# One small load split over two issuing queues, in a kernel that streams 285 MB

## The chip, the cores and the metric

The kernel runs on one core of a Trainium2 chip. The metric is the time of one execution on the device in microseconds. The profile gives a span, from the first to the last instruction, which is about 1.7 us shorter. Faster or slower would need a difference of 2%, 13 us.

## The reference

```python
def setup_inputs():
    B, H, W = 4, 4224, 4224
    return {"x": np.random.randn(B, H, W).astype(np.float32)}

def reference(x):
    ps = np.cumsum(np.cumsum(x, axis=1), axis=2)
    diag = np.diagonal(ps, axis1=1, axis2=2)
    return np.cumsum(diag, axis=1).astype(np.float32)
```

Each element of x has to be read once: 285.47 MB. The output is 4 x 4224 numbers.

## The kernel before

Strips of 768 rows (6 per partition) are loaded by GpSimd, which casts them from fp32 to bf16 on the way. There are three strip buffers. Each strip is summed along rows (VectorE and ScalarE) and along columns (TensorE). The last 384 rows of the last matrix are handled by blocks of 128 rows, and their last 384 columns, the *head*, are loaded first of all, in fp32, by SyncE.

```python
    HC = GW                      # 384
    NH = N - HC
    src = x[LB, T0:N, :].rearrange("(h p) w -> p h w", p=P)
    src_a = src[:, 0:2, :]
    head = last.tile([P, F, HC], FP32, name="head")        # F = 3 blocks
    nc.sync.dma_start(out=head, in_=src[:, :, NH:N])
    ...
    prefetched = []
    for i in range(NBUF):        # 3 strips ahead
        t = strip_tile()
        load_rows(t, 0, i * F2 * P)                        # nc.gpsimd.dma_start
        prefetched.append(t)
    ...                          # constants: some 25 GpSimd instructions
    row_sums(hs, head)           # the head's first reader, on VectorE
    for h in range(F):
        w = GW - h * P
        masked(hmu[:, h, :w], head[:, h, HC - w :], um1[:, :w], hu[:, h : h + 1])
    ...
    # then for each strip: mask, subtract, row sums (VectorE), column sums (TensorE)
```

Of the kernel before, what the change touches and what calls it, by code (L numbers as in the profile page):

```python
# [17 lines left out]
def kernel(  # L18
# [15 lines left out]
    nc = tc.nc  # L34

    B, H, W = x.shape
    N = H
# [31 lines left out]
    NH = N - HC  # L69
    src = x[LB, T0:N, :].rearrange("(h p) w -> p h w", p=P)  # L70
    src_a = src[:, 0:2, :]
    head = last.tile([P, F, HC], FP32, name="head")
    nc.sync.dma_start(out=head, in_=src[:, :, NH:N])

    def strip_tile():
        return strips.tile([P, F2, N], BF16, name="strip")
# [21 lines left out]
    def upper_mask(f, c0):  # L98
# [17 lines left out]
        out=um1,  # L116
        in_=um1,
# [13 lines left out]
        out=ident,  # L131
        in_=ident,
# [30 lines left out]
    def between_groups(name, n, turned):  # L163
# [39 lines left out]
        out=weights,  # L203
        in_=weights,
# [12 lines left out]
        out=steps, in_=steps, scalar=2, op=ALU.arith_shift_right  # L217
# [84 lines left out]
    for b in range(B):  # L302
# [90 lines left out]
        if not whole:  # L393
# [9 lines left out]
            for sb, c0, c1 in (  # L403
# [8 lines left out]
                    out=part_b[:, sb, c0:c1],  # L412
                    in_=x[b, r0 : r0 + R, :NH].rearrange("r (k c) -> r k c", k=4)[
                        :, :, c0:c1
                    ],
# [23 lines left out]
        for i, src in enumerate((d, c12[:, 0, :])):  # L439
            nc.vector.tensor_tensor_scan(  # L440
                out=c12[:, i, :],
# [6 lines left out]
        if whole:  # L448
# [4 lines left out]
            out=out[b, :T0].rearrange("(g i) -> g i", i=GW), in_=c12[1:, 1, :]  # L453
# [60 lines left out]
        for k in (1, 0, 2):  # L514
# [3 lines left out]
            out=out[b, T0 : T0 + E0].unsqueeze(0), in_=yl[:, :E0]  # L518
# [34 lines left out]
```

## Time and profile before

| | before |
|---|---|
| time, first three runs | 667.07 us median (667.06 to 667.53) |
| span | 665.4 us |
| read from HBM | 285.47 MB |
| transfer engines busy, 2 to 662 us | full (share 1.01) |
| first byte | 1.8 to 2.0 us |
| head: issued, landed, first read | 0.82, 4.8, 20.27 us |
| last strip data landed | 662.3 us |

The lines behind this table stand in the prediction. Read such a page from the DMA row: as it is full in every slice here, an instruction on another engine can matter only if it moves the beginning or the end of the stream, or makes a hole in it.

### The profile page before, as it was taken

The page shows a single profiled execution, that of the slowest core. Times are in us where ns is not written, and L with a number is a line of the kernel's source. Part 1 is how long each engine was busy: PE and PEld are TensorE (multiplying, and loading weights), DVE is VectorE, ACT ScalarE, POOL GpSimd, SP SyncE. Part 2 cuts the span into 40 slices and gives each one's busy share as a digit, 9 for nine tenths or more (in the row PEclk, how much of TensorE's full clock was granted, in tenths as well). Part 3 has the DMA queues.
Part 4 walks back from the last instruction along what each step waited for, and adds up shares of the span by engine and source line. Part 5 has one row for each costly group of instructions (what it writes and reads, how often), then busy time and mean ns, then how long its engine had stood idle before and what let it go on. Part 6 is the DMA issues. An engine that isn't in the chain of part 4 may idle for free.

```text
span 665.4 us, 2461 instructions
## 1 busy us (share of the span) xinstructions
PE 201.7 (30%) x948; PEld 103.7 (16%) x948; DVE 326.4 (49%) x136; ACT 136.9 (21%) x222; POOL 31.8 (5%) x62
## 2 busy tenths in 40 slices
PE   0081423402007143140200623404032163250418
PEld 0040211201004021120100312202011031120103
DVE  3261625456906153454780524436388243352767
ACT  0001121406300103040630020304063002030434
POOL 6100000000000000000000000000000000001000
PEclk9995857656558585666755957666565586766758
DMA  9999999999999999999999999999999999999998
GB/s 206 219 219 219 219 219 215 212 210 218 219 218 219 219 220 218 218 213 212 216 218 218 217 219 219 218 219 211 215 216 219 219 214 220 216 219 216 214 208 162
DMA packets 7631, 143.25 MB, mean 215 GB/s; under 512 B 536, under 2 KB 1604, under 8 KB 2116
## 3 DMA queue, kind: packets, MB, share of 16 engines
q0 software_dynamic: 7152, 142.44, 99.9%
q1 hardware_dynamic: 468, 0.66, 0.3%
q8 instruction: 7, 0.11, 0.1%
q14 instruction: 4, 0.03, 0.0%
HBM read 285.47 MB, written 0.07 MB: 429 GB/s over the span
## 4 chain that ended last, share of the span: by engine, by line
another core or an unknown queue 44%; DVE 42%; DMA 11%; issue 1%; POOL 0%; PE 0%; DVEq 0%; POOLq 0%
DVE acc L246 27%; DMA strip<-in_x_dram 11%; DVE mu L333 7%; DVE strip L334 7%; DVE c L440 0%; POOL strip L411 0%; DVE rows L348 0%; PE d L226 0%; POOL strip L400 0%; DVE pu L246 0%; PE fin_e L226 0%; DVE c L266 0%; DVE pair L255 0%; PE carry_ps L226 0%
## 5 line engine op out<-in xcount | busy, mean ns | idle before, releaser
L226 PE MATMUL d<-strip,sel 128*33 128x384 bf16 (+1 forms) x603 | 140.7, 408 | 397.9 <-DMA strip<-in_x_dram 397.9
L241 ACT ACTIVATE dump<-strip 128x416 bf16<-128x416 bf16 (+6 forms) x110 | 125.1, 1138 | 520.5 <-DMA strip<-in_x_dram 517.8
L333 DVE TENSOR_TENSOR mu<-strip,um 128x4608 bf16<-128x4608 bf16 (+1 forms) x24 | 52.4, 2183 | 316.4 <-DMA strip<-in_x_dram 316.3
L246 DVE TENSOR_REDUCE acc<-strip 128x6 f32<-128x4608 bf16 (+6 forms) x23 | 196.0, 8523 | 0.8
L226 PEld LDWEIGHTS <-sel 128*33 128x33 bf16 (+1 forms) x849 | 94.9, 112 | 534.1 <-issue 495.9
L226 PE MATMUL d<-mu,sel 128*33 128x384 bf16 (+1 forms) x243 | 48.9, 353 | 45.4 <-DVE mu L333 45.4
L334 DVE TENSOR_TENSOR strip<-strip,mu 128x4608 bf16<-128x4608 bf16 (+1 forms) x24 | 52.4, 2183 | 1.0
L80 POOL DMA_DIRECT2D strip<-in_x_dram x24 | 16.5, 687 | 536.7 <-DVE acc L246 312.3
L241 ACT ACTIVATION_READ_ACCUMULATOR dump<-strip 128x1 f32 x110 | 20.5, 186 | 0.0
L226 PE MATMUL fold<-strip,ident_h 128*128 128x480 bf16 x8 | 3.4, 601 | 10.8 <-DMA strip<-in_x_dram 10.8
L96 DVE MEMSET um<- 128x6144 bf16 x1 | 5.2, 5178 | 1.2 <-issue 1.2
L216 DVE TENSOR_SCALAR steps<-steps 128x128 int32<-128x128 int32 x1 | 0.2, 227 | 11.0 <-POOL steps L215 11.0
L101 POOL TENSOR_SCALAR_AFFINE_SELECT um<-um 128x4608 bf16<-128x4608 bf16 (+1 forms) x2 | 5.2, 2614 | 4.0 <-DVE um L96 4.0
L226 PEld LDWEIGHTS <-ident_h 128*128 128x128 bf16 x21 | 2.2, 113 | 14.8 <-issue 13.8
L411 POOL DMA_DIRECT2D strip<-in_x_dram x5 | 2.7, 552 | 26.5 <-DMA strip<-in_x_dram 26.5
L226 PE MATMUL d<-ones_all,rows 128*33 128x128 f32 (+1 forms) x12 | 2.3, 347 | 5.4 <-DVE rows L348 5.4
L226 PE MATMUL fold_a<-strip,ident_h 128*128 128x512 bf16 x13 | 3.3, 380 | 0.3 <-DMA strip<-in_x_dram 0.3
L246 DVE TENSOR_REDUCE parts<-strip 128x3 f32<-128x3072 bf16 x1 | 3.4, 3352 | 0.0
L400 POOL DMA_DIRECT2D strip<-in_x_dram x2 | 1.4, 714 | 30.8 <-DVE acc L246 30.8
L226 PEld LDWEIGHTS d<-halves,rows 128*33 128x33 f32 (+1 forms) x24 | 2.5, 150 | 0.7 <-issue 0.5
L226 PE MATMUL d<-halves,rows 128*33 128x64 f32 (+1 forms) x24 | 2.6, 284 | 0.0
L348 DVE TENSOR_TENSOR rows<-acc 64x30 f32<-64x30 f32 (+2 forms) x12 | 2.1, 177 | 0.9
(80 smaller groups left out, 34.7 us busy)
## 6 DMA issues: line engine op xcount, KB each, us to landing
strip<-in_x_dram POOLq DMA_DIRECT2D x19, 6336.0 KB, 76.6
strip<-in_x_dram POOLq DMA_DIRECT2D x5, 3168.0 KB, 59.8
strip<-in_x_dram POOLq DMA_DIRECT2D x1, 1152.0 KB, 50.2
strip<-in_x_dram POOLq DMA_DIRECT2D x1, 768.0 KB, 53.3
strip<-in_x_dram POOLq DMA_DIRECT2D x3, 240.0 KB, 54.3
head<-in_x_dram SPq DMA_DIRECT2D x1, 576.0 KB, 4.0
strip<-in_x_dram POOLq DMA_DIRECT2D x1, 176.0 KB, 43.2
strip<-in_x_dram POOLq DMA_DIRECT2D x1, 64.0 KB, 28.6
```

Source lines behind the costliest of these rows:

```text
L80: nc.gpsimd.dma_start(out=o, in_=x[b, r0 : r0 + f * P, :].rearrange("(p f) w -> p f w", f=f))
L96: nc.vector.memset(um_all, 1.0)
L101: nc.gpsimd.affine_select(out=um, in_=um, compare_op=ALU.is_gt, fill=0.0, base=0, pattern=[[-1, f], [1, f * P]], channel_multiplier=-f,)
L216: nc.vector.tensor_single_scalar(out=steps, in_=steps, scalar=2, op=ALU.arith_shift_right)
L226: nc.tensor.matmul(o, lhsT=lhsT, rhs=rhs, start=start, stop=False, skip_group_check=True)
L241: nc.scalar.activation(out=dump[:, :w], in_=src, func=ACT.Copy, accum_out=acc)
L246: nc.vector.reduce_sum(out=acc, in_=src, axis=AX.X)
L333: nc.vector.tensor_mul(out=mu, in0=block, in1=um)
L334: nc.vector.tensor_sub(out=block, in0=block, in1=mu)
L348: nc.vector.tensor_add(out=o, in0=acc[..., 0], in1=acc[..., 1])
L400: nc.gpsimd.dma_start(out=part_a[:, :, c0:c1], in_=src_a[:, :, c0:c1])
L411: nc.gpsimd.dma_start(out=part_b[:, sb, c0:c1], in_=x[b, r0 : r0 + R, :NH].rearrange("r (k c) -> r k c", k=4)[:, :, c0:c1],)
```

## The change

The intent is to spread the first load over two sequencers (the parts of SyncE and ScalarE that issue loads), so that issuing and landing overlap: row blocks 0 and 1 by SyncE, block 2 by ScalarE, which has nothing to do at that time.

```diff
     head = last.tile([P, F, HC], FP32, name="head")
-    nc.sync.dma_start(out=head, in_=src[:, :, NH:N])
+    nc.sync.dma_start(out=head[:, 0:2, :], in_=src[:, 0:2, NH:N])
+    nc.scalar.dma_start(out=head[:, 2, :], in_=src[:, 2, NH:N])
```

## The prediction

> **What bounds the kernel now.** I read the page first: the row of DMA busy shares in 40 slices, the GB/s row, the queue table and the HBM line.
>
> ```profile
> span 665.4 us, 2461 instructions
> ...
> DMA  9999999999999999999999999999999999999998
> GB/s 206 219 219 219 219 219 215 212 210 218 219 218 219 219 220 218 218 213 212 216 218 218 217 219 219 218 219 211 215 216 219 219 214 220 216 219 216 214 208 162
> ...
> q0 software_dynamic: 7152, 142.44, 99.9%
> q1 hardware_dynamic: 468, 0.66, 0.3%
> ...
> HBM read 285.47 MB, written 0.07 MB: 429 GB/s over the span
> ```
>
> The reader is to see that the transfer engines are at 90% or more in every slice but the last, and that almost all of it is one queue, the casting strip loads that GpSimd issues. The queue that the change touches (q1, SyncE's loads and stores) holds 0.66 MB of 143.25 MB and 0.3% of the engines' time. The GB/s row counts bytes written into the core's memory: a strip is read as 4 bytes and written as 2, so 219 written is 438 read. The input, 4 x 4224 x 4224 x 4 bytes = 285.47 MB, is exactly what the page says was read: each element is read once, and there is nothing to save.
>
> Second, stretches of time at both ends, to see when the transfers begin and stop (columns: stretch, length, busy times of PE, PEld, DVE, ACT and POOL, clock, DMA share, GB/s).
>
> ```profile
> 1.60:1.80 0.20, 0.00 (x0) 0.00 (x0) 0.00 (x0) 0.20 (x1) 0.20 (x1) 1.00 0.00 0
> 1.80:2.00 0.20, 0.00 (x0) 0.00 (x0) 0.00 (x0) 0.20 (x1) 0.20 (x1) 1.00 0.20 61
> 2.00:2.20 0.20, 0.00 (x0) 0.00 (x0) 0.00 (x0) 0.10 (x1) 0.20 (x2) 1.00 1.44 169
> ...
> 2.00:662.00 660.00, 200.76 (x937) 103.05 (x937) 325.05 (x128) 135.07 (x220) 30.93 (x58) 0.66 1.01 217
> ```
>
> No byte moves before 1.8 us; from 2 us to 662 us the share is 1.01, that is full. So the time is about 1.9 us to the first byte, 660.4 us of streaming, and the rest to the end. 285.47 MB in 660.4 us is 432.3 GB/s.
>
> Third, the chain of waits, its first transfer and its end (start, length, what), and two lines of the list of who waited for whom (total, times, longest).
>
> ```profile
> 1.33 33.28 DMA strip<-in_x_dram
> ...
> 619.08 43.23 DMA strip<-in_x_dram
> 662.33 0.40 DVE pair L255 x2
> ```
> ```profile
> DVE mu L333 <- DMA strip<-in_x_dram: 316.3, 20, 19.8
> POOL strip L80 <- DVE acc L246: 312.3, 10, 32.2
> ```
>
> The chain gives VectorE 42% of the span, because each new strip load is issued when VectorE has released a buffer. This is not the bound: VectorE then waits 316.3 us for strips, and GpSimd waits for it only with other strips already queued (a strip load lands 76.6 us after its issue, 2.5 times the 30 us that one strip streams). The queue never runs dry, as the row of nines says. The chain ends in a strip transfer that lands at 662.33 us; 3.1 us of finishing work follow.
>
> Fourth, the timeline of the start, for the first load itself, and the list of issues for its landing (KB each, us to landing).
>
> ```profile
> 0.81 1.28 ACT L241 ACT_TABLE_LOAD   x1 [0.81 <-PEq L537]
> 0.82 0.45 SPq L73 DMA_DIRECT2D head<-in_x_dram  x1
> ...
> 1.33 2.27 POOL L80 DMA_DIRECT2D strip<-in_x_dram  x3 [0.81 <-POOLq L537]
> ...
> 20.27 1.31 DVE L246 TENSOR_REDUCE hs<-head 128x3 f32<-128x1152 f32 x1
> ...
> 34.64 2.56 DVE L333 TENSOR_TENSOR mu<-strip,um 128x4608 bf16<-128x4608 bf16 x1 [11.82 <-DMA strip<-in_x_dram]
> ```
> ```profile
> head<-in_x_dram SPq DMA_DIRECT2D x1, 576.0 KB, 4.0
> ```
>
> The head is issued at 0.82 us and has landed 4.0 us later, at 4.8 us. Its first reader, the row sum on VectorE, starts at 20.27 us with no wait in brackets: it comes after constants that GpSimd was making until 19.1 us. Head data has lain ready for 15.5 us. ScalarE does a table load and then nothing until the first strip lands at 34.6 us.
>
> **What the Trainium skill says.** "DMA: Bandwidth & Descriptors", section "Issuing engines are not separate DMA queues": loads from SyncE, ScalarE and GpSimd run on the same 16 transfer engines, and issuing from several "will only save the time on the sequencer". The trace of before has SyncE's head and GpSimd's strips both moving in the first microseconds, but cannot yet test two such hardware queues. Same page, "Where 436 GB/s comes from": a fabric ceiling of 435.2 GB/s. The 432.3 GB/s worked out above is 99.3% of it: agreement, and nothing left to gain in rate. Same page, "Latency and other measured facts": first byte about 0.6 us for loads issued from SyncE or ScalarE. Here the issue ends at 0.82 + 0.45 = 1.27 us and bytes appear between 1.8 and 2.0 us, so 0.5 to 0.7 us after the end of the issue, or about 1.1 us after its start. "Perfetto Trace Analysis", section "Summary: the profiler window per engine type": the window of such an issue leaves out the data movement. The trace agrees: 0.45 us of window against 4.0 us to landing.
>
> **The change part by part.**
> 1. Removed: one load of 128 x 3 rows of 384 floats (384 runs of 1,536 bytes, 576 KB) from SyncE. Added: one of 256 runs (384 KB) on SyncE, one of 128 runs (192 KB) on ScalarE. Bytes and run length are the same; 0.59 MB at 432 GB/s is 1.4 us of the engines' time in both kernels. Difference in streaming time: 0.
> 2. SyncE's issue: if the 0.45 us were wholly proportional to runs it would become 0.30 us, if fixed it stays 0.45. Nothing else is on SyncE before 517 us. What could matter is only whether the first byte comes sooner: by at most 0.15 us, and this counts only because for a moment the head has the engines to itself (GpSimd's first strip issue lasts from 1.33 to about 2.1 us).
> 3. ScalarE's issue: by the same row 0.3 to 0.45 us, ahead of or behind its table load of 1.28 us (0.81 to 2.09 us). If ahead, the table load ends at about 2.5 us; first use at 34.6 us, slack 32 us. If behind, the third block is issued at 2.1 us and lands by about 2.1 + 4.0 = 6.1 us; first use at 20.27 us, slack 14 us. On the path: 0 in either case.
> 4. Landing of the head: perhaps half a microsecond sooner or later than 4.8 us. The row sum needs all three blocks and still starts at about 20.3 us. On the path: 0.
> 5. Waits: the row sum now waits for two completions, and the end of the program may have one more queue to settle. The last waits of SyncE at the end are 0.2 us each; I put 0 to 0.2 us here, as an estimate from those.
> Sum: -0.15 to +0.2 us, centre 0. 667.07 + 0.03 gives 667.1 us.
>
> **The rivals.**
> - The start gets faster: two sequencers share the issuing, the engines fill sooner, and everything behind moves up. For it: the stream is continuous, so a microsecond gained at the start would come through to the end whole. Against: GpSimd's strips are ready for the engines from about 2 us anyway, and no byte can be moved before the issue and the latency to first byte, which both kernels have. Gain at most 0.15 us: 666.9 us.
> - The two hardware queues beside the strips' queue hold back the first strip: three queues in turn, not two, so a smaller part for strips while the head is moving. For it: the head and strips overlap. Against: the head ends sooner by as much as it takes, and the stream only cares for the sum of bytes. The first strip might land at 34.6 plus or minus 0.5 us; with full queues behind it the end stays. 667.1 us.
> - A fixed price for the first use of ScalarE's queue, at start or end, outside the span: the measured time is 1.7 us more than the span (667.14 against 665.4), which is the size of all such work that before has. One more queue could add some tenths: 667.5 us. Nothing in the profile of before can show it.
> - The head comes late, with VectorE's start held up: it would have to land 15 us later to be seen at all, and another 12 us (the 11.82 us of idle time before the first strip) to reach the strips. Excluded in practice.
>
> **Range and chances.** The three runs of before lie from 667.06 to 667.53 us, so 0.5 us of scatter is ordinary. Adding the -0.15 to +0.5 us of the rivals and a little for another chip or moment (0.1%, 0.7 us, a guess), I take 666.3 to 668.2 us. A step of 2% is 13.3 us, more than nine times the time of all the head's bytes, and nothing here can make it: chances 0.01 faster, 0.98 within 2%, 0.01 slower, the ends left for a disturbed run.
>
> **What would show it right or wrong.** Right: HBM read still 285.47 MB; the row of nines as before; two head issues at about 0.8 us, from SyncE and ScalarE, both landed before 7 us; the row sum of the head at 20.3 us with no wait on a transfer; first strip work at 34.6 us, within 0.5; the last strip landing at 662.3 us, within 0.5. Wrong: a slice with a hole in the DMA row; a strip landing late by the same amount all through; a wait on the head before the row sum; or a span that stays while the measured time rises, which would be the queue's fixed price. A first byte clearly before 1.8 us with the last landing earlier by as much would speak for the first rival.

## The result, and the profile after

The changed kernel took 667.93 us in the median of six runs (667.03 to 668.64), the kernel before 667.18 us in six runs (667.06 to 667.53). The ratio is 1.0009, with a 95% interval from 0.9996 to 1.0022: no difference. (A ratio here is the mean time of one kernel's fast runs over the mean of the other's of the same rounds, so not quite the ratio of the two medians.) The profiled run took 667.05 us, with a span of 665.3 us. The gap between time and span is 1.7 us, as before.

The page after, DMA row, queues (packets, MB, share of the engines' time) and HBM line:

```profile
span 665.3 us, 2463 instructions
...
DMA  9999999999999999999999999999999999999998
...
q1 hardware_dynamic: 340, 0.46, 0.2%
q10 hardware_dynamic: 144, 0.20, 0.2%
...
HBM read 285.47 MB, written 0.07 MB: 429 GB/s over the span
```

A new queue, q10, has taken 0.20 MB from q1. Its 144 packets are 128 runs of the head and 16 more of a few bytes: q1 went from 468 to 340, the total from 7631 to 7647. The DMA row and the bytes read are unchanged.

The timeline of the start, and the first reader of the head and of a strip:

```profile
0.82 0.45 SPq L73 DMA_DIRECT2D head<-in_x_dram  x1
0.82 0.41 ACTq L74 DMA_DIRECT2D head<-in_x_dram  x1
...
1.26 1.28 ACT L242 ACT_TABLE_LOAD   x1 [1.26 <-PEq L538]
1.33 2.27 POOL L81 DMA_DIRECT2D strip<-in_x_dram  x3 [0.81 <-POOLq L538]
...
20.27 1.31 DVE L247 TENSOR_REDUCE hs<-head 128x3 f32<-128x1152 f32 x1
...
34.71 2.56 DVE L334 TENSOR_TENSOR mu<-strip,um 128x4608 bf16<-128x4608 bf16 x1 [11.88 <-DMA strip<-in_x_dram]
```

Both issues begin at 0.82 us. SyncE's takes as long for 256 runs as it took for 384 (0.45 us), and ScalarE needs 0.41 us for 128. ScalarE's table load has moved back by 0.45 us, which delays nothing. The row sum of the head starts at 20.27 us as before.

The landing of the two parts (KB, us from issue), and the two strip transfers at the ends of the chain of waits:

```profile
head<-in_x_dram SPq DMA_DIRECT2D x1, 384.0 KB, 4.1
head<-in_x_dram ACTq DMA_DIRECT2D x1, 192.0 KB, 3.3
```
```profile
1.33 33.35 DMA strip<-in_x_dram
...
618.98 43.22 DMA strip<-in_x_dram
```

The whole head is there at 4.9 us, against 4.8 before: two queues have not brought it sooner. The first strip landed at 34.68 us against 34.61, the last at 662.20 against 662.31 (start and length added, as in the lines above and in those of the prediction).

### The profile page after: what moved, and what is told of

Read it like the earlier page. It is cut to its first block, busy times and chain, and to the rows that moved or that the text cites. A ratio compares the mean times of both kernels' runs of the same rounds, so it can differ in the third digit from the quotient of the medians.

```text
span 665.3 us, 2463 instructions
## 1 busy us (share of the span) xinstructions
PE 197.0 (30%) x948; PEld 101.8 (15%) x948; DVE 326.4 (49%) x136; ACT 136.9 (21%) x222; POOL 31.8 (5%) x62
## 4 chain that ended last, share of the span: by engine, by line
another core or an unknown queue 44%; DVE 42%; DMA 12%; issue 1%; POOL 0%; PE 0%; DVEq 0%; POOLq 0%
DVE acc L247 27%; DMA strip<-in_x_dram 12%; DVE strip L335 7%; DVE mu L334 7%; DVE c L441 0%; POOL strip L412 0%; DVE rows L349 0%; PE d L227 0%; POOL strip L401 0%; DVE pu L247 0%; PE fin_e L227 0%; DVE c L267 0%; DVE pair L256 0%; PE carry_ps L227 0%
## 5 line engine op out<-in xcount | busy, mean ns | idle before, releaser
L227 PE MATMUL d<-strip,sel 128*33 128x384 bf16 (+1 forms) x603 | 137.0, 400 | 401.1 <-DMA strip<-in_x_dram 401.1
L227 PEld LDWEIGHTS <-sel 128*33 128x33 bf16 (+1 forms) x849 | 93.3, 110 | 534.9 <-issue 494.9
L227 PEld LDWEIGHTS d<-ones_all,rows 128*33 128x33 f32 (+1 forms) x12 | 1.4, 131 | 6.8 <-DVE rows L349 5.6
```

Of the source, the lines that this page charges most:

```text
L227: nc.tensor.matmul(o, lhsT=lhsT, rhs=rhs, start=start, stop=False, skip_group_check=True)
```

## The experiments

What was left to explain: whether the 0.75 us between the two medians is real, and whether the time follows the bytes of the head, its landing, or something else. My theory was that of the prediction (a full stream; the head's 1.4 us of bytes cost the same in both kernels, and its landing time costs nothing). The rivals were a price of ScalarE's queue, a price of an additional load, and transfer time at the start that lies idle and hides the head. Eleven runs of kernels were made, each timed in five rounds beside the kernel before.

| run | median, us | lowest to highest, us | ratio to before, 95% interval |
|---|---|---|---|
| before against itself | 668.10 | 667.50 to 669.07 | 1.0005 (0.9991 to 1.0019) |
| changed, again | 667.17 | 667.04 to 668.27 | 0.9998 (0.9985 to 1.0010) |
| changed, third time | 667.17 | 667.11 to 667.38 | 0.9994 (0.9980 to 1.0007) |
| split on SyncE alone | 667.03 | 666.95 to 669.24 | 0.9997 (0.9984 to 1.0010) |
| whole head on ScalarE | 667.34 | 666.99 to 668.42 | 0.9999 (0.9986 to 1.0011) |
| 1.18 MB more at the start | 670.29 | 670.23 to 670.37 | 1.0034 (1.0021 to 1.0046) |
| head issued at 20 us | 668.87 | 668.76 to 668.99 | 1.0013 (0.9999 to 1.0027) |
| no head load | 667.10 | 666.90 to 667.30 | 0.9992 (0.9979 to 1.0004) |
| head on GpSimd's queue | 668.31 | 668.16 to 668.67 | 1.0011 (0.9998 to 1.0023) |
| strips after the head | 670.73 | 670.68 to 670.95 | 1.0047 (1.0035 to 1.0060) |
| first strip's load cut in two | 667.33 | 667.16 to 668.07 | 0.9996 (0.9982 to 1.0009) |

### Are the 0.75 us real?

The kernel before against itself, with no edit:

> The kernel before against itself, to see what scatter a comparison has here. Every theory: ratio 1.000, interval within 0.001 on either side, median 667.1 to 667.3 us. If it comes out at 1.001 (667.9) as the changed kernel did, that 0.75 us is drift and belongs to no kernel.

The changed kernel again and a third time, with no edit:

> The changed kernel again, unaltered. Theory (the load lies off the path, the time is the stream of bytes): ratio 1.000 within 0.0005, median 667.0 to 667.4 us. Rival (ScalarE's queue has a fixed price that four of the six first runs paid): ratio 1.001 to 1.0015, median about 667.9 us, again in two groups (667.0 and 668.2).

> The changed kernel a third time, on whatever chip this is, for the two groups: theory: best runs 667.0 to 667.1, others 1 to 2 us above, as with before; in its profile the work on the first strip and the last transfer are late by the same amount against the best run (34.7 and 662.3 us).

The kernel before, against itself, came out at 1.0005, with a median of 668.10 us for five runs and 667.71 us for the nine beside them. The changed kernel came out at 0.9998 and 0.9994. So the 0.75 us belong to no kernel. Over all comparisons the changed kernel ran 16 times, from 667.03 to 668.64 us with a median of 667.19; the kernel before ran 47 times, from 667.01 to 669.32 us with a median of 667.53. The best runs agree within 0.02 us. Both kernels have runs of 1 to 2 us more, those of before on all three chips, and the expectation of an interval of 0.001 either side was too narrow.

### A price of the queue, or of one more load?

```diff
 # split on SyncE alone
+    nc.sync.dma_start(out=head[:, 0:2, :], in_=src[:, 0:2, NH:N])
+    nc.sync.dma_start(out=head[:, 2, :], in_=src[:, 2, NH:N])
 # whole head on ScalarE
+    nc.scalar.dma_start(out=head, in_=src[:, :, NH:N])
```

> The same split into two blocks and one, both issued by SyncE one after the other; ScalarE issues nothing. Theory: 667.1 us, ratio 1.000. Rival of the queue's price: also 667.1, as no new queue is used. Rival of the additional load (16 more completion packets, two semaphores for the row sum): 667.9 us, ratio 1.001. In the trace the second issue should follow the first by 0.45 us, so the third block lands later than with ScalarE, at about 5 us, still 15 us ahead of its reader.

> The whole head as one load from ScalarE, none from SyncE at the start. Theory: 667.1 us, ratio 1.000, head landed about 4.0 us after its issue, table load of ScalarE moved from 0.81 to 1.26 us. Rival of the queue's price: 667.9 us or more, ratio 1.001, as ScalarE's queue is used and now for all the head's bytes. Rival of the additional load: 667.1 us.

Best runs 666.95 and 666.99 us: neither the new queue nor the additional load has a price that can be seen (the intervals reach some 0.9 us to either side). The two parts on SyncE were issued at 0.82 and 1.31 us, and each landed 3.3 us after its issue, the last at 4.6 us; with ScalarE's help it was 4.9 us, and 4.7 us in the second profile of the changed kernel.

The profiled run of the split on SyncE is worth a look, as it took 669.24 us, while the four timed ones took 666.95 to 667.18. Its chain of waits:

```profile
1.33 35.83 DMA strip<-in_x_dram
...
621.19 43.22 DMA strip<-in_x_dram
```

The first strip landed at 37.16 us, 2.5 us later than in the runs of 667 us, and the last strip data at 664.41, 2.2 us later. All that was lost was lost before the first strip was in. The last microseconds show how (stretches; the last two columns are the share of the 16 engines and GB/s), first of this run, then of the changed kernel at 667.05 us:

```profile
662.50:663.00 0.50, 0.42 (x2) 0.17 (x3) 0.35 (x3) 0.50 (x2) 0.00 (x0) 1.00 0.14 24
663.00:663.50 0.50, 0.50 (x6) 0.39 (x5) 0.00 (x0) 0.12 (x2) 0.00 (x0) 1.00 0.11 19
663.50:664.00 0.50, 0.50 (x8) 0.40 (x6) 0.46 (x3) 0.40 (x1) 0.00 (x0) 1.00 0.08 14
664.00:664.50 0.50, 0.50 (x9) 0.41 (x6) 0.38 (x2) 0.25 (x3) 0.00 (x0) 1.00 0.08 11
```
```profile
662.00:662.50 0.50, 0.41 (x7) 0.18 (x4) 0.43 (x2) 0.30 (x2) 0.00 (x0) 1.00 0.10 13
662.50:663.00 0.50, 0.33 (x6) 0.21 (x6) 0.50 (x5) 0.32 (x2) 0.00 (x0) 1.00 0.00 0
```

One engine of 16 is a share of 0.06. In the slower run about one engine worked alone from 663.5 us on, and the others had finished. In the faster run all were done by 662.5. So a strip is there when the last of 16 engines has its part, and one late engine makes the whole run late.

The transfer records of the packed traces bear this out. They don't name the engine, but a strip's packet (25,344 bytes written) follows the one before it on its engine without a gap, 1.89 us each, so 16 chains can be told apart. This is when the 11th packet of a chain ended: the spread over the 16 chains and the last of them, beside the time of the same run. The last three rows are of runs described below.

| profiled run | spread, us | last end, us | time, us |
|---|---|---|---|
| changed, third time | 0.47 | 25.03 | 667.17 |
| before | 0.52 | 25.02 | 667.14 |
| changed | 0.60 | 25.06 | 667.05 |
| before against itself | 1.19 | 25.98 | 668.20 |
| whole head on ScalarE | 1.74 | 26.31 | 668.42 |
| changed, again | 1.91 | 26.38 | 668.15 |
| split on SyncE | 2.93 | 27.52 | 669.24 |
| no head load | 1.04 | 25.14 | 667.16 |
| head on GpSimd's queue | 0.73 | 26.26 | 668.32 |
| strips after the head | 0.86 | 28.59 | 670.68 |

The time follows the last end: in all ten runs it is 641.7 to 642.2 us more, while the last ends lie 3.6 us apart. The spread alone misleads: without the head it is 1.04 us and nothing is lost, because there the other engines are early and the last one is not late. In the split on SyncE the last engine's first strip packet began at 6.17 us (on the others at 3.6 to 4.3 us), though all packets of the head had ended by 4.29 us on every engine; and in all four slower runs of the first seven the last engine's first strip packet took 2.7 to 2.9 us in place of 1.89.

### What the head's bytes cost

```diff
 # 1.18 MB more at the start: a second load behind the head, into a buffer overwritten later
     nc.sync.dma_start(out=head, in_=src[:, :, NH:N])
+    extra = mup.tile([P, F2, F2 * P], BF16, name="mu6")
+    nc.sync.dma_start(out=extra.bitcast(FP32), in_=x[0, 0:F2 * P, 0:HC].rearrange("(f p) w -> p f w", p=P))
```

> Before, with a second load behind the head on SyncE: 768 runs of 1,536 bytes, 1.18 MB, twice the head's bytes, into a buffer that is overwritten before it is used (results stay right). Theory (bytes count, landing times do not): 1.18 MB at 432.3 GB/s is 2.7 us, so 669.9 us, ratio 1.0041, the whole stream shifted by 2.7 us and no hole in the DMA row. Rival (the start has idle transfer time that hides small loads): under 0.5 us, 667.1 to 667.6 us. Rival (short runs are dearer than their bytes): over 4 us, 671 us or more.

670.29 us, all five runs within 0.14 us, and 3.0 us above the lowest run of before on the same chip (667.25). Bytes alone would make 2.7 us. By the records a packet of 1,536 bytes takes 65 to 78 ns on an engine, and 768 / 16 = 48 of them make 3.1 to 3.7 us, an estimate; the 3.0 us lie between the two reckonings. Taken alone, this run spoke for the prediction and against the rival of idle time at the start. The run without a head, below, shows why it could not tell: the head itself already fills that time. The extra load landed 55.1 us after its issue, and VectorE, which needed that buffer, began on the first strip at 56.56 us in place of 34.64. That lateness of 22 us is not seen in the time.

```diff
 # head issued at 20 us: its load waits for a write that GpSimd makes after its constants
-    nc.sync.dma_start(out=head, in_=src[:, :, NH:N])
     ...
+    nc.gpsimd.memset(head, 0.0)
+    nc.sync.dma_start(out=head, in_=src[:, :, NH:N])
     asum = last.tile([P, 2, 4], FP32, name="asum")
```

> Before, with the head's load held back until GpSimd has made its constants (it writes the head's tile first, so the load waits for it), at about 19 us, in the midst of the strip stream. Theory: the same bytes in the same stream, so as long as the head lands before VectorE's other work runs out of buffers the time stays 667.1 us, ratio 1.000; VectorE's row sum of the head is then held up by a wait for the head that the trace shows, and if this goes past 34.6 us the first strip's work comes late, which the three buffers should absorb up to about 30 us. Rival (the first strip's work is on the path): the time grows by as much as the first strip's work is late. If the head takes turns with the strips' large packets on each engine it could land some 10 to 50 us after its issue; 4 us if not.

The issue list and the timeline of this run, VectorE's row sum with the wait before it and its first work on a strip:

```profile
head<-in_x_dram SPq DMA_DIRECT2D x1, 576.0 KB, 48.0
```
```profile
68.14 1.35 DVE L245 TENSOR_REDUCE hs<-head 128x3 f32<-128x1152 f32 x1 [46.97 <-DMA head<-in_x_dram]
...
70.65 2.55 DVE L334 TENSOR_TENSOR mu<-strip,um 128x4608 bf16<-128x4608 bf16 x1
```

In the midst of the strip stream the head needed 48.0 us to land, not 4. On each engine its 24 packets take turns with strip packets: 24 x (1.89 + 0.08) = 47 us. VectorE began on the first strip 36 us late. Yet the time was 668.87 us, only 1.8 us above the 667.10 us of the next run, which has no head load; 24 packets of 78 ns are 1.9 us. (In its records the last of the 16 chains ended its 11th packet at 24.96 us, and the time is 643.8 us more, not 642: again 1.8 us, put in after the start.) So even here the time follows what the engines have to move, and 36 us of lateness are absorbed by the buffers. But the expected ratio of 1.000 was wrong: bytes that cost nothing at the start cost 1.8 us here.

```diff
 # no head load: results of the last blocks wrong on purpose
-    nc.sync.dma_start(out=head, in_=src[:, :, NH:N])
     ...
+    nc.gpsimd.memset(head, 0.0)
```

> Before without the head's load at all: GpSimd fills the head's tile with zeros, so the last row blocks come out wrong on purpose. Theory of the prediction (the head's 0.59 MB cost 1.4 us of the stream wherever they lie): 667.1 - 1.4 = 665.7 us at best. New theory after the late-head run (the strips' own first packets start only at about 2.8 us, and the head fills engine time that would lie idle): 666.6 to 667.2 us at best. Theory on the scatter (one of the 16 engines now and then starts its strips late while the head's packets are in its way, and the whole stream ends late by that): without the head's load the five runs agree within 0.4 us. Rival on the scatter (the chip or the strips alone): they spread over 1 us or more, as before does.

This run decides it: 667.10 us with no head at all, 666.90 at best, against 667.01 at best for before. The prediction's 1.4 us for the head's bytes would have made it 665.7. The medians of the same rounds differ by more, 667.10 against 667.75 us, and the interval (0.9979 to 1.0004) would by itself allow 1.4 us; but the runs of before include late engines, so I compare the best runs, and the two profiled runs at 667.14 and 667.16 us. (The comparison with the reference passed in spite of the zeros, presumably because the head's part is small beside sums over the whole matrix; so that comparison doesn't guard the head.) Stretches at the start, without the head:

```profile
2.60:2.80 0.20, 0.00 (x0) 0.00 (x0) 0.20 (x1) 0.00 (x0) 0.20 (x1) 1.00 0.00 0
2.80:3.00 0.20, 0.00 (x0) 0.00 (x0) 0.20 (x1) 0.00 (x0) 0.20 (x2) 1.00 7.40 1140
```

GpSimd's strips, issued at 1.32 us, move nothing before 2.8 us. (A long packet is booked in the stretch in which it begins, hence a share over 1.) Bytes of the head move from 1.8 us on. Moreover, the records show that the first strip packet on each engine takes 2.6 us in the median here, where it takes 1.89 us in the kernel before, in which the head has gone ahead of it. So about 0.9 + 0.7 = 1.6 us of each engine's time is there for the head, which needs 24 x 65 to 78 ns = 1.6 to 1.9 us. This is an account by sums, and the chains of packets add to it: on the middle one of the 16 engines the 11th strip packet ended at 24.29 us without the head and at 24.75 with it, on the last one at 25.14 and 25.02. So the head cost most engines about 0.5 us, and nothing on the last one, which sets the time. The first strip's work began at 34.81 us without the head and at 34.64 us with it.

### What of the start counts in full

```diff
 # head on GpSimd's queue, ahead of the strips
-    nc.sync.dma_start(out=head, in_=src[:, :, NH:N])
+    nc.gpsimd.dma_start(out=head, in_=src[:, :, NH:N])
 # strips after the head
     nc.sync.dma_start(out=head, in_=src[:, :, NH:N])
+    probe = last.tile([P, 1], FP32, name="probe")
+    nc.gpsimd.tensor_copy(out=probe, in_=head[:, 2, HC - 1 : HC])
```

> The head issued by GpSimd ahead of the strips, on their queue; SyncE and ScalarE issue nothing at the start. If the idle time before 2.8 us is what the head uses up, this costs the head's own time: 1.4 to 1.9 us above the best runs of before and up to 0.8 us for GpSimd's additional issue ahead of the strips, 668.4 to 669.8 us. If the queue doesn't matter: 667.1 us. Scatter: small, below 0.4 us, if it comes from two queues meeting on an engine.

> Before, but GpSimd reads one column of the head before it issues the first strip, so the strips start when the head has landed, at about 3.5 to 4.8 us. Head and strips never meet on an engine at the start. Stream: later by some 2 to 3 us, 669 to 670.5 us at best. Scatter, if it comes from the meeting: below 0.4 us. If it has another cause: 1 us or more.

On GpSimd's queue the head cost 1.2 us against no head (668.31 against 667.10), a little less than the 1.3 to 2.7 us that I expected: it began at 2.8 us as the strips would have done, and the strips' first issue came 0.9 us later. The timelines show when the strips were issued, first without a head, then with the strips held back until the head was there:

```profile
1.32 2.27 POOL L79 DMA_DIRECT2D strip<-in_x_dram  x3 [0.81 <-POOLq L537]
```
```profile
4.80 0.19 POOL L75 COPY probe<-head 128x1 f32<-128x1 f32 x1 [4.27 <-DMA head<-in_x_dram]
4.92 1.55 POOL L82 DMA_DIRECT2D strip<-in_x_dram  x2
```

4.92 us against 1.32 us is 3.6 us later, and 670.73 against 667.10 us is 3.6 us longer; more than the 2 to 3 us that I expected. So the strips' first issue is on the path: these 3.6 us came through whole, and the head's issue is not on it.

The scatter was nearly gone in the runs in which head and strips did not meet at the start (head late, no head, head on the strips' queue, strips after the head): 20 runs, each kernel's five within 0.51 us. Of the 47 runs of before, 22 were above 667.6 us. But the run with more bytes at the start was within 0.14 us though there they meet, and the third group of the changed kernel within 0.27 us. So the late engine seems to have to do with how the start is laid out, which no run isolates. I had expected the head's packets to be in its way; the split on SyncE, where they had all ended 1.9 us before the late engine's first strip packet began, speaks against that. What makes it late remains open.

### A version that beats both?

```diff
 # first strip's load cut in two
-            load_rows(t, 0, i * F2 * P)
+            nc.gpsimd.dma_start(out=t[:, 0:1, :], in_=rows0[:, 0:1, :])   # for i == 0
+            nc.gpsimd.dma_start(out=t[:, 1:, :], in_=rows0[:, 1:, :])
```

> A try for a version that beats both: before, with the first strip's load cut in two (one row of each partition's six, then the other five), so that GpSimd's first and smaller load may be written out sooner and the strips start before 2.8 us. From the run with the strips issued 3.6 us later, which ended 3.6 us later, the first issue counts in full: if the smaller load takes 0.55 us to issue where the whole one takes 0.75, best runs 666.8 to 666.9 us. Rival (the head fills the time before the strips' first packets, so an earlier start of the strips only displaces the head): 667.0 to 667.1 at best, as before. Rival (runs of 16.9 KB in place of 101 KB, and one more issue): 667.3 us or more at best.

667.16 us at best against 667.20 of before on that chip. GpSimd's first issue took 0.66 us, not 0.55. Nor did the strips start sooner: by the records of its profiled run (668.07 us) their first packet began at 3.96 us, in before at 3.83. So the earlier start that this run was to test did not come about, and what one would be worth is not shown. Nothing is gained, and I have found no version that beats either kernel. With the head removed altogether the best time falls by 0.1 us only; what else it takes away is scatter.

## Why the prediction was right or wrong

The predicted 667.1 us and "within 2%" held: 667.93 us in the first six runs lies in the range, and 667.19 us over all 16.

1. *Streaming time, difference 0*: right. Bytes and the DMA row are the same, and the last strip data landed within 0.1 us of before.
2. *SyncE's issue, 0.30 to 0.45 us*: it is 0.45. The issue is not in proportion to the runs (0.45 us for 384 and for 256, and 0.46 us for 128 in the split on SyncE), so no first byte could come sooner; it is at 1.8 to 2.0 us in both.
3. *ScalarE's issue ahead of its table load, slack of 32 us*: right, as the timeline shows.
4. *Landing within half a microsecond of 4.8 us, off the path*: right (4.9 us), and the late head shows how far off: 48 us to land, and 36 us of lateness not seen.
5. *More to wait for, 0 to 0.2 us*: nothing can be seen; the gap of time and span stayed at 1.7 us.

Two terms were mis-sized without harm to the result. The 1.4 us of engine time for the head's bytes was put into both kernels; at the start it measures 0.1 us between the best runs, in the midst of the stream 1.8 us. As it stood in both kernels, its error cancelled, and the predicted difference did not depend on it. The step that failed is the sentence in the first rival, that the strips "are ready for the engines from about 2 us anyway": alone they start at 2.8 us, and behind the head at 3.8 us. And the scatter of "0.5 us" came from three runs; 47 runs spread over 2.3 us. With the range cut to that first scatter, the median of the first six runs would have been missed.

One reading of the prediction is not shown either. It finds 432.3 GB/s in agreement with a ceiling of 435.2 GB/s, which its page states for the ports of the core's memory. The 432.3 count bytes read; 217 GB/s were written into that memory. That the engines are busy throughout is shown (share 1.01), but not that this ceiling is what limits them.

The rival of three queues in turn named the right place, for it is in the first microseconds that an engine can fall behind. But this occurs in before as well (22 of 47 runs above 667.6 us, against 6 of 16 of the changed kernel), so nothing marks it as an effect of the third queue.

## What to carry to other kernels

In a kernel with a full stream, ask of each load at the start whether it delays the stream's first issue (3.6 us later cost 3.6 us here), and not how fast it lands itself; a small load on a quicker queue before the stream gets going cost 0.1 us between the best runs here, and the same load in the middle cost 1.8 us. To know what a load costs, take it away: the run without the head was worth more than any split of it. Before a difference of a microsecond is explained, run the kernel against itself, and look at when the last of the transfer engines ends.

## What the Trainium skill lacked or had wrong

- "DMA: Bandwidth & Descriptors", section "Queues, rings and completion order", says that an engine takes turns between queues packet by packet. The late head agrees (24 turns beside packets of 1.89 us, 47 us worked out, 48.0 us measured). But the section gives some 9 to 17 descriptors as typical of a packet, where a turn here moved one run of 1,536 bytes; and it lacks the consequence: a small load with short runs, issued into a stream of long ones, took 12 times as long as at the start.
- The same page, "Specifications", gives 512 bytes as the least transfer for line rate. Here runs of 1,536 bytes took 78 ns beside the stream, 19.7 GB/s on an engine (65 ns at the start, 23.6 GB/s), where a strip packet reads 50,688 bytes in 1.886 us, 26.9 GB/s, all counted in bytes read.
- No page that I read shows how one late engine of 16 looks in a profile: there is no hole in the DMA row, only a share near 0.06 in the last microseconds. In the split on SyncE the first strip landed 2.5 us late, the last strip data 2.2 us late, and the run took 669.24 us against 667.1 us.
- No page that I read says whether the issue of a load grows with its runs: SyncE's took 0.45 us for 384 and for 256 runs and 0.46 us for 128, ScalarE's 0.42 us for 384 and 0.41 us for 128, so splitting a load shortens no issue.
